# Eight-core hybrid decoder: list-scheduled engines, tiled input and output, block-Toeplitz convolution, folded pooling maps, sums of squares on GpSimd

## The chip, the cores and the metric

The kernel runs on the 8 cores of one Trainium2 chip. Each core handles one sequence of the batch (2048 tokens of 1024 channels), with no exchange between cores. The metric is the device time of the slowest core, in microseconds (us). Each core has TensorE (PE, with the weight loads as PEld), VectorE (DVE), ScalarE (ACT), GpSimd (POOL) and SyncE (SP). They run their own instruction streams and meet through semaphores.

The programs of this case have a second, slower state: in some executions some cores show a lower granted TensorE clock and take longer. In one execution of the kernel before, for instance, cores 4 to 7 had a clock of 0.80 and took 4486 to 4497 us; the other four had 0.966 to 0.971 and took 3822 to 3835.

## The reference, cut to what matters

```python
def reference(x, ...):                         # x (8, 2048, 1024) float32, one sequence per core
    for i in range(4):                         # mixers in order A, B, C, A
        h = rmsnorm(x, norm_mix[i])            # x / sqrt(mean(x*x) + eps) * g
        x = x + mixer[i % 3](h)
        x = x + channel_mlp(rmsnorm(x, norm_mlp[i]), m_w1[i], m_w2[i])   # relu(h@w1)^2 @ w2, 1024->4096->1024
    return rmsnorm(x, norm_final)
# A: z = gelu(h @ w_in + b_in), u and v of 3072 each; v = layernorm(v);
#    gate = causal 128x128 map in chunks of 128 tokens, 8 groups; (u * gate) @ w_out
# B: p = h @ w_in; trailing means over 2, 4, 8, 16 tokens minus p; a 256x256 map per group; @ w_out
# C: a, g = h @ w_in; y = a * sigmoid(g); causal depthwise convolution, 31 taps; layernorm; silu; @ w_out
```

Nine norms of the whole sequence are needed, each in four tiles of 512 tokens. Each of these 36 tile norms stands before some matmuls.

## The kernel before

x stays in SBUF for the whole program, transposed (channels on partitions), as 8 blocks `kc` times 4 tiles `tt` of 128x512 float32. PE transposes x at the beginning and the result at the end. The order of the work is the order of the program text, with look-ahead placed by hand. A tile norm sums its squares on PE: ACT squares a block into bf16, and a matmul with a matrix of 1/1024 adds it up in PSUM (the accumulation memory that matmuls write) and spreads it over all partitions.

```python
def rms_rstd(rb, tt, dst=None, dst_res=None):
    # ... (cut)
    for kc in range(KC):                                      # 8 blocks
        sq, sqr = next_sq()
        sc.op("act", I("activation", out=sq[:], in_=xT[:, kc, t0:t0 + 512], func=AF.Square), ...)
        sc.op("pe", I("matmul", bk[:], lhsT=onesm[:], rhs=sq[:], start=(kc == 0), stop=(kc == KC - 1)), ...)
    sc.op("act", I("activation", out=sd, in_=bk[:], func=AF.Sqrt, bias=epst[:, 0:1], scale=1.0), ...)
    sc.op("dve", I("reciprocal", out=sd, in_=sd), rd=[], wr=[sdr])

def rmsnorm(rb, tt, gcol, out_fn, out_res_fn):
    sd, sdr = rms_rstd(rb, tt)
    for kc in range(KC):                                      # both inputs, x and sd, lie in SBUF
        sc.op("dve", I("scalar_tensor_tensor", out=o, in0=xT[:, kc, t0:t0 + 512],
            scalar=pv[:, gcol + kc:gcol + kc + 1], in1=sd, op0=ALU.mult, op1=ALU.mult), ...)

# mixer A, V: 8 matmuls and a ninth for the bias, then gelu on ACT
fns.append(I("matmul", bk[:], lhsT=sel1[:], rhs=brow[:, vp * 512:(vp + 1) * 512], start=False, stop=True))

# mixer C, convolution: 31 matmuls with diagonal matrices per 128 channels and 512 tokens
fns = [I("matmul", bk[:], lhsT=dg[di][:, k, :], rhs=yext[:, dc, 2 + k:2 + k + 512], start=(k == 0), stop=(k == CK - 1))
       for k in range(CK)]
# ... (input transposes, mixer B, MLP, layer norm of C cut)
```

## Time and profile before

Five runs had a median of 3835.2 us; four lie between 3832.8 and 3838.1, and one took 4102.9. The page of the profile (busy time of each engine, share of the span, instructions) and its chain of work that ended last begin so:

```profile
PE 3595.2 (94%) x16792; PEld 1640.7 (43%) x16792; DVE 2160.1 (56%) x2926; ACT 1069.8 (28%) x1627; POOL 242.6 (6%) x293
...
PE 84%; DVE 7%; ACT 3%; issue 3%; DMA 3%; DVEq 0%; ACTq 0%; SPq 0%; POOLq 0%
```

PE is the bound: 94% busy and 84% of the chain. GpSimd is nearly idle. The next lines are the windows of the slowest core: from:to and length in us, then busy time and instructions of each engine, the granted TensorE clock, the DMA share and the GB/s. They show the start, the first mixer A, the first MLP, mixer B and mixer C.

```profile
0.00:83.00 83.00, 38.44 (x197) 30.80 (x197) 35.03 (x39) 19.27 (x32) 7.34 (x30) 0.76 0.83 174
83.00:652.00 569.00, 553.86 (x2807) 259.49 (x2807) 257.19 (x395) 206.12 (x269) 72.34 (x78) 0.98 0.94 127
652.00:1128.00 476.00, 463.67 (x2101) 206.51 (x2100) 306.14 (x438) 109.56 (x177) 14.29 (x17) 0.99 0.26 42
1128.00:1306.00 178.00, 145.17 (x599) 60.42 (x597) 107.30 (x98) 56.81 (x90) 18.12 (x21) 0.89 0.72 105
...
1776.00:2247.00 471.00, 427.28 (x1830) 180.14 (x1829) 264.92 (x206) 137.96 (x214) 19.88 (x23) 0.95 0.34 52
```

"Busy" is not the same as "at the peak". In back-to-back stretches a bf16 matmul of 512 columns starts every 215.8 ns and one of 128 columns every 55.8 ns. Counting every matmul at these durations (and the float32 ones at theirs) gives 3462 us of PE work that cannot shrink while the instructions stay. The other 375 us of the span are waits and slow restarts after waits. (A restart in this trace: after a wait of 2.75 us, 32 matmuls took 8.75 us instead of 7.07. The granted clock was 0.54 in their first 3.4 us and 1.00 again 5 us after they began.) I call the two parts work and waiting.

Groups, by line, engine, operation, tile and shape (busy us, mean ns of one, then idle time before them and its releaser):

```profile
L79 PE MATMUL bank<-c_yext,c_dg_67 128*128 128x512 bf16 x496 | 117.6, 397 | 12.4 <-DVE c_dg_67 L79 12.4
L79 DVE TENSOR_SCALAR m_hT<-xT,pv 128x512 bf16<-128x512 f32 x128 | 53.2, 488 | 0.6 <-ACT rsq_16 L79 0.2 <-ACT rsq_14 L79 0.2
L79 DVE SCALAR_TENSOR_TENSOR hTp_22<-xT,pv,rsd_20 128x512 bf16<-128x512 f32 x64 | 43.1, 746 | 1.1 <-DVE rsd_20 L79 0.3 <-PE bank L79 0.2
```

The first is half of the 992 diagonal matmuls of the convolution. The other two are the scalings of a norm on DVE: 488 ns with one SBUF tile as input, 746 ns with two (x and the reciprocal root).

### The profile page before, as it was taken

What the parts mean: (1) busy time and instruction counts of PE and PEld (TensorE: products, weight loads), DVE (VectorE), ACT (ScalarE), POOL (GpSimd) and SP (SyncE); (2) the same over time, 40 slices, a digit from 0 to 9 for tenths busy, and PEclk for the clock granted to TensorE, in tenths of its full rate; (3) what the DMA queues carried; (4) which work ended last, traced back from release to release, by engine and by line L of the source; (5) the groups of instructions that cost most, each with busy time, mean ns of one, the idle gap of its engine ahead of it and who ended that gap; (6) DMA issues with size and microseconds to landing.
All of it is one profiled execution on the core that took longest, in us unless ns stands there. A gap on an engine that the chain in (4) does not pass through costs nothing.

```text
span 3837.2 us, 48293 instructions; the slowest of 8 cores (3820.4 to 3837.2 us)
## 1 busy us (share of the span) xinstructions
PE 3595.2 (94%) x16792; PEld 1640.7 (43%) x16792; DVE 2160.1 (56%) x2926; ACT 1069.8 (28%) x1627; POOL 242.6 (6%) x293
## 2 busy tenths in 40 slices
PE   5999998999998799999998989999799999899997
PEld 3444444444443244444333434444344444344444
DVE  4446434655567565666455566566544543465656
ACT  2433332211133221112223241112253423221113
POOL 0111111000001000000000000000001111100000
PEclk7999999999999899999999999999899999999999
DMA  7889999121237422224222422222289999912212
GB/s 151 122 117 136 147 133 135 24 45 34 35 58 108 75 34 34 45 39 72 44 34 35 64 44 45 34 34 44 39 121 123 128 154 129 133 23 45 38 19 88
DMA packets 302325, 283.88 MB, mean 74 GB/s; under 512 B 4870, under 2 KB 281478, under 8 KB 302088
## 3 DMA queue, kind: packets, MB, share of 16 engines
q0 software_dynamic: 295104, 262.16, 47.7%
q1 hardware_dynamic: 6988, 18.64, 1.5%
q8 instruction: 143, 2.34, 0.3%
q14 instruction: 90, 0.74, 0.1%
HBM read 534.54 MB, written 8.39 MB: 141 GB/s over the span
## 4 chain that ended last, share of the span: by engine, by line
PE 84%; DVE 7%; ACT 3%; issue 3%; DMA 3%; DVEq 0%; ACTq 0%; SPq 0%; POOLq 0%
PE bank L79 84%; DVE m_hT L79 1%; DMA ring_9<-a_w_out 1%; DVE hTp_22 L79 1%; DVE xT L79 1%; ACT b_pooled L79 0%; DVE c_dg_66 L79 0%; DVE c_rstd L79 0%; DMA xin_31<-x 0%; DVE b_tA L79 0%; DVE rsd_20 L79 0%; ACT rsq_16 L79 0%; DVE c_dg_67 L79 0%; ACT L79 0%; ACT rsq_14 L79 0%
## 5 line engine op out<-in xcount | busy, mean ns | idle before, releaser
L79 DVE TENSOR_TENSOR xT<-bank,xT 128x512 f32<-128x512 f32 x1152 | 787.0, 690 | 434.4 <-PE bank L79 429.8
L79 DVE BATCH_NORM_STATS2 a_stats<-a_v 128x6 f32<-128x512 bf16 x192 | 129.5, 690 | 184.1 <-ACT a_v L79 183.8
L79 PE MATMUL bank<-m_hT,ring_10 128*128 128x512 bf16 x896 | 207.2, 391 | 14.9 <-DVE m_hT L79 13.7
L79 PE MATMUL bank<-m_hT,ring_9 128*128 128x512 bf16 x896 | 204.1, 387 | 6.7 <-DVE m_hT L79 6.7
L79 ACT ACTIVATE a_uT<-bank,pv 128x512 bf16<-128x512 f32 x192 | 129.5, 689 | 203.1 <-PE bank L79 203.0
L79 ACT ACTIVATE a_v<-bank 128x512 bf16<-128x512 f32 x192 | 114.6, 597 | 244.4 <-PE bank L79 244.2
L79 PE MATMUL bank<-m_hT,ring_11 128*128 128x512 bf16 x768 | 174.3, 386 | 7.0 <-DVE m_hT L79 7.0
L79 PE MATMUL bank<-m_hT,ring_12 128*128 128x512 bf16 x768 | 169.7, 379 | 0.0
L79 PE MATMUL bank<-m_hT,ring_13 128*128 128x512 bf16 x768 | 169.7, 379 | 0.0
L79 PEld LDWEIGHTS bank<-m_hT,ring_10 128*128 128x128 bf16 x896 | 89.3, 100 | 127.8 <-issue 29.5
L79 PEld LDWEIGHTS bank<-m_hT,ring_9 128*128 128x128 bf16 x896 | 89.1, 100 | 116.6 <-issue 16.0
L79 PE MATMUL bank<-c_yext,c_dg_67 128*128 128x512 bf16 x496 | 117.6, 397 | 12.4 <-DVE c_dg_67 L79 12.4
L79 ACT ACT_TABLE_LOAD x43 | 55.2, 1283 | 263.7 <-PE bank L79 228.0
L79 PEld LDWEIGHTS bank<-m_hT,ring_11 128*128 128x128 bf16 x768 | 76.1, 99 | 101.2 <-issue 14.0
L79 PE MATMUL bank<-c_yext,c_dg_66 128*128 128x512 bf16 x496 | 112.7, 385 | 5.0 <-DVE c_dg_66 L79 5.0
L79 PEld LDWEIGHTS bank<-m_hT,ring_12 128*128 128x128 bf16 x768 | 75.2, 98 | 90.6
L79 PEld LDWEIGHTS bank<-m_hT,ring_13 128*128 128x128 bf16 x768 | 75.1, 98 | 90.3
L79 ACT ACTIVATE a_v<-a_v,a_nmr,a_sdv 128x3072 bf16<-128x3072 bf16 x32 | 94.3, 2947 | 22.1 <-DVE a_nmr L79 22.1
L79 PE MATMUL bank<-hTp_22,ring_12 128*128 128x512 bf16 x352 | 83.9, 386 | 6.8 <-ACT a_uT L79 6.8
L79 PEld LDWEIGHTS bank<-c_yext,c_dg_67 128*128 128x128 bf16 x496 | 49.7, 101 | 78.2 <-issue 24.3
L79 PE MATMUL bank<-a_uT,ring_9 128*128 128x512 bf16 x360 | 82.6, 379 | 0.0
L79 PE MATMUL bank<-hTp_22,ring_13 128*128 128x512 bf16 x320 | 75.4, 384 | 7.3 <-ACT hTp_22 L79 7.3
(352 smaller groups left out, 5826.1 us busy)
## 6 DMA issues: line engine op xcount, KB each, us to landing
ring_10<-a_w_in POOLq DMA_DIRECT2D x20, 1024.0 KB, 15.2
ring_11<-a_w_in POOLq DMA_DIRECT2D x20, 1024.0 KB, 12.3
ring_12<-a_w_in POOLq DMA_DIRECT2D x20, 1024.0 KB, 16.1
ring_13<-a_w_in POOLq DMA_DIRECT2D x19, 1024.0 KB, 12.8
ring_9<-a_w_in POOLq DMA_DIRECT2D x17, 1024.0 KB, 18.0
ring_10<-m_w POOLq DMA_DIRECT2D x14, 1024.0 KB, 8.7
ring_9<-m_w POOLq DMA_DIRECT2D x13, 1024.0 KB, 8.3
ring_11<-m_w POOLq DMA_DIRECT2D x13, 1024.0 KB, 8.4
```

Source lines behind the costliest of these rows:

```text
L79: return lambda e: getattr(e, _method)(*args, **kwargs)
```

## The change: intent and core of the diff

The kernel was rewritten. The intent: take off PE what another engine can do, shorten what has to stay, and let a scheduler on the host fix the order of each engine's instructions from modelled durations, so that PE rarely waits.

- x and the output come in tiles that are already transposed, so there are no float32 transposes on the chip.
- Sums of squares: ACT squares in float32, GpSimd adds the 8 blocks (7 adds of 128x512), and PE does one float32 matmul.
- The bias of V is a DVE add in PSUM instead of a ninth matmul.
- Convolution as block-Toeplitz matrices: 384 matmuls of 128 columns and 256 bf16 transposes instead of 992 full matmuls. Mixer C's scalings write straight into the order that this needs.
- Mixer B's group map is multiplied into its output map once.
- The normalisation of v goes from ACT to DVE.

```diff
-        for kc in range(KC):                                     # in rms_rstd
-            sc.op("act", I("activation", out=sq[:], in_=xT[:, kc, t0:t0 + 512], func=AF.Square), ...)
-            sc.op("pe", I("matmul", bk[:], lhsT=onesm[:], rhs=sq[:], start=(kc == 0), stop=(kc == KC - 1)), ...)
+        for kc in range(KC):                                     # in sum_squares
+            sc.op("act", I("activation", out=sq[:], in_=xs(kc, tt), func=AF.Square), ...)
+            if kc:
+                last = kc == KC - 1
+                sc.op("pool", I("tensor_tensor", out=acc if last else sacc[:], in0=sacc[:], in1=sq[:], op=ALU.add), ...)
+    sc.op("pe", MM(bk.v(), onesr[:], acc1[:], True, True), ..., cost=c_pe(1), tag="rms")     # in rms
...
-                        fns.append(I("matmul", bk[:], lhsT=sel1[:], rhs=brow[...], start=False, stop=True))
+                        sc.op("dve", I("tensor_tensor", out=bk.v(), in0=bk.v(), in1=bvb[:, vp * 512:(vp + 1) * 512], op=ALU.add), ...)
...
-            for k in range(CK): ... lhsT=dg[di][:, k, :], rhs=yext[:, dc, 2 + k:2 + k + 512]
+            # in words: c_T (128x1536, built from the taps and a mask, half on DVE, half on GpSimd) times transposed y, 128 columns each
...
+    def schedule(self):                                          # in Sched, on the host
+        while done < n:
+            for e in self.ENGS:                                  # of the ops that are ready on each engine
+                ... cand.append((max(rt, t0), i))                # take the one that can start first
+        o.end = s + cost + (0.12 if e == "pe" else 0.06)         # modelled end
```

## The prediction

> **What bounds it now.** The page (part 1) has PE busy for 3595 of 3837 us (94%), and the chain of waits is 84% PE; DVE is at 56%, ACT 28%, POOL 6%. In an MLP stretch (stage windows) 1730 matmuls of 128x512 take 375 us at granted clock 1.00: 216 ns each. Mixer A's 128-column matmuls in a row come at 56 ns. With the program's counts: 15650 full matmuls (3377 us), 768 short ones (43), float32 input/output transposes (64), mixer A's set-up (28): 3512 us of PE work. The other 325 us is waiting or half-clock restarts: V begins only at 82.9 us (timeline), each mixer-to-MLP change loses about 20 us, mixer B about 50 of 181, the second A set-up 25, the tail 30.
>
> **PE work removed** (estimates from those durations)
> - Convolution: 992 full matmuls become 384 of 128 columns plus 256 bf16 transposes: -178 us.
> - Norm sums, 8 matmuls per tile to 1: -51. Mixer C's LN sums: -14.
> - V's 192 bias matmuls go to DVE: -41.
> - float32 transposes go to the host: -64. A set-up: -24. B's group map: -3.
>
> Sum -375: about 3138 us of PE work remain. Nearly all of it was on the critical path.
>
> **Added elsewhere.** DVE gets 192 bias adds (0.69 us) and v's normalisation (ACT took 2.95 us each), and loses memsets and the 4.3 us diagonal builds. GpSimd gets about 250 adds of 128x512. [...] GpSimd also issues the weight loads (0.88 us each) in order.
>
> **Waits that stay or come**
> - Start: x tile 0 (2 MB) lands near 14 us, then squares, adds, 3.35 us reciprocal, 8 scalings of 0.75: V at about 29 us.
> - Tail: the same chain and the store, about 22 us after the last matmul.
> - Mixer C starts only when all tiles are ready; its end (statistics, transposes, re-read of spilled x, an MLP that needs all of x) leaves PE waiting about 25 us.
> - Mixer B about 15, stage changes 3 to 8 each. A tile of mixer A loads 18.9 MB; the backlogged queue moved 157 GB/s (120 us) and PE will need 135, so DMA nearly binds: some us per layer.
>
> A gap of 3 us also costs 1.8 us of half-clock matmuls (32 took 8.75 instead of 7.07 us). Gaps in all about 75.
>
> **Time.** 3138 + 29 + 22 + 75 = 3264: **3265 us, 8 in 10 between 3205 and 3360**. Faster by over 2%: 0.98; within 2%: 0.015; slower: 0.005.
>
> **What would show it.** PE instructions about 15600; PE busy about 3190 us, 97%; matmuls still 216 ns, clock about 0.98; MLP layers about 445 us each; V's first matmul near 29 us; POOL busy from 243 to 600 us or more; mixer C about 235 us (505 before); mixer B under 140 us; DVE busy not above 2300 us.
>
> **What would make it wrong.** [...] in-order GpSimd holding back weight loads; mixer A bound by DMA; mixer C's end serialised on DVE; a static schedule whose modelled order blocks an engine[...].

The sum came to 3138 + 29 + 22 + 75 = 3264. Of the 29, x at 14, the reciprocal of 3.35 and 8 scalings of 0.75 make 23.4; the other 5.6 (squares, adds, the sum on PE) were the author's estimate.

## The result, and the profile after

The kernel after took 3418.9 us (median of five; four runs between 3416.0 and 3419.0) against 3835.2 us. The ratio is 0.891 (95% interval 0.890 to 0.893). A ratio here is the mean time of one kernel's runs over that of the other's runs of the same rounds, so it is not quite the ratio of the medians. Executions over 1.5% slower than the fastest of the same kernel are left out of the means. The direction was right. The time lies 154 us above the predicted 3265 and outside the range (3205 to 3360).

The fifth run, the one that was profiled, took 8749.9 us, with granted clocks of 0.41 to 0.57 on four cores (the other four had 1.00 and took 7591 to 8211 us). The first experiment ran the same kernel again, and the lines below are from that execution (3412.0 us, all cores at clock 0.975 to 0.977).

> The changed kernel once more, unedited, because its only profile fell in an execution of 8750 us with granted clocks down to 0.41. If that execution is a disturbance of the chip, this one takes about 3419 us with a clock of 0.97 on all cores, and its trace shows where the 154 us over the predicted 3265 us lie. If the kernel itself provokes it, it appears here again.

It was fast and correct, so the long execution was a disturbance and not a property of the kernel. The page after (engines, chain):

```profile
PE 3185.4 (93%) x15640; PEld 1480.1 (43%) x15640; DVE 2228.1 (65%) x3222; ACT 913.8 (27%) x1460; POOL 664.8 (19%) x572
...
PE 85%; DVE 6%; issue 4%; POOL 1%; DMA 1%; SPq 1%; ACT 1%; DVEq 0%; POOLq 0%; ACTq 0%
```

PE's busy time fell by 410 us, as predicted, but its share is 93% and not 97%: the span fell by 428 us, and the waits were not nearly gone. The windows of the same stages:

```profile
0.00:84.00 84.00, 22.00 (x77) 9.16 (x78) 22.57 (x26) 24.98 (x39) 37.51 (x50) 0.88 0.98 191
84.00:600.00 516.00, 507.85 (x2629) 241.24 (x2628) 338.58 (x533) 162.05 (x249) 102.23 (x99) 1.00 1.07 142
600.00:1055.00 455.00, 443.56 (x2048) 200.35 (x2046) 296.87 (x408) 109.48 (x181) 59.81 (x56) 1.00 0.27 42
1055.00:1206.00 151.00, 118.44 (x565) 52.15 (x564) 133.09 (x121) 42.53 (x73) 97.91 (x67) 0.88 0.50 77
...
1652.00:1933.00 281.00, 229.07 (x1478) 125.61 (x1479) 184.08 (x369) 92.36 (x153) 89.64 (x53) 0.91 0.35 70
```

Mixer A and the MLP are within reach of their work. The start (84 us), B (151) and C (281) are not; there the granted clock averages 0.88 to 0.91. The clock record of this trace drops to 0.5 around gaps: from 60.8 to 81.3 us, for instance, where PE stood from 56 to 76.5 us. The waits of PE, by what ended them (us in total, times, longest):

```profile
PE bank L159 <- POOL acc L159: 44.7, 9, 24.7
PE bank L159 <- DVE xT L159: 25.6, 8, 6.8
PE bank L159 <- DVE hT L159: 23.2, 2, 15.3
PE bank L159 <- ACT a_v L159: 20.4, 1, 20.4
PE bank L159 <- DVE c_h L159: 20.3, 1, 20.3
PE bank L159 <- DVE b_pl L159: 19.6, 3, 13.2
PE bank L159 <- DVE c_z L159: 16.7, 2, 15.0
```

The names: `acc` is the GpSimd sum of a norm, `hT` its scaled result, `c_h` the scaled input of mixer C, `a_v` the gelu of V, `b_pl` the pooled tile of B and `c_z` the normalised tile of C. Work and waiting of this trace, counted as before, against the terms of the prediction:

| term | predicted, us | measured, us |
|---|---|---|
| PE work | 3138 | 3135 |
| waiting at the start (predicted: V's first matmul) | 29 | 67 |
| after the last MLP matmul | 22 | 28 |
| waiting in between, restarts included | 75 | 179 |
| sum | 3264 | 3409 |

The 179 us are: mixer A 10 and 23, the MLPs 14, 5, 8 and 12, mixer B 41, mixer C 67. Each figure is the length of a stage less its work. The span of this execution is 3409 us; the median of the five runs is 9 us longer.

Now the groups that answer to those of before (columns as there):

```profile
L159 DVE TENSOR_TENSOR xT<-bank,xT 128x512 f32<-128x512 f32 x1120 | 764.2, 690 | 409.6 <-PE bank L159 397.8
L159 POOL TENSOR_TENSOR sacc<-sacc,sq 128x512 f32<-128x512 f32 x216 | 290.3, 1344 | 262.2 <-ACT sq L159 203.5 <-ACT sacc L159 29.7 <-POOL sacc L159 24.4
L159 DVE SCALAR_TENSOR_TENSOR hT<-xT,pv,rs 128x512 bf16<-128x512 f32 x96 | 98.0, 1086 | 0.3 <-DVE rs L159 0.2
L159 DVE TENSOR_SCALAR mh<-xT,pv 128x512 bf16<-128x512 f32 x128 | 79.8, 652 | 2.7 <-DVE xT L159 0.5
L159 PE MATMUL bank<-c_T,c_yT 128*128 128x128 bf16 x384 | 26.2, 231 | 5.4 <-POOL c_T L159 5.4
```

The new convolution is as short as predicted. But the scalings of the same shape went from 746 to 1086 ns (`hT`) and from 488 to 652 (`mh`, before `m_hT`). These are means of two kinds. Counted one by one in this trace, the 54 `hT` scalings with no GpSimd instruction beside them took 742 ns, and the 42 with one took 1529 ns. For `mh` it is 478 ns (79) and 933 ns (49). The residual adds `xT<-bank,xT`, which read one operand from PSUM and one from SBUF, kept their 690 ns, beside GpSimd (688, 225 of them) as alone (692). DVE itself is not slower; in these groups it depends on what the instruction reads and on what runs beside it. A stretch of the start shows how (start us, us, engine, operation, tiles; the first line merges the 8 scalings of a tile):

```profile
29.84 10.61 DVE L159 SCALAR_TENSOR_TENSOR hT<-xT,pv,rs 128x512 bf16<-128x512 f32 x8 [0.17 <-DVE rs L159]
...
34.44 1.47 POOL L159 TENSOR_TENSOR sacc<-sacc,sq 128x512 f32<-128x512 f32 x1 [0.20 <-POOL sacc L159]
```

Of these 8 scalings, five took 1.74 or 1.75 us. Each of the five ended 0.54 or 0.55 us after the GpSimd add beside it ended (the add above ended at 35.91 us, its scaling at 36.46). A stretch of mixer B's timeline shows the same on a very small instruction:

```profile
1079.85 2.26 DVE L159 TENSOR_TENSOR b_t<-b_t,invc 128x2 f32<-128x2 f32 x1
1080.12 1.96 POOL L159 TENSOR_TENSOR b_t<-b_px 128x1054 f32<-128x1054 f32 x1
...
1090.84 0.15 DVE L159 TENSOR_TENSOR b_t<-b_t,invc 128x6 f32<-128x6 f32 x1
```

A DVE instruction on two columns lasted 2.26 us and ended as the GpSimd instruction beside it ended. A like one on six columns, later, took 0.15 us. The profile counts the stretched time as busy time of DVE. I call this stretching *the port*, as the edits below do; the word is only a name, and no run shows what in the chip causes it. The trace shows which instructions it meets: of those with two SBUF inputs, `hT` (742 ns alone, 1529 beside GpSimd) and the two-column one (2.26 us); of those with one, `mh` (478 and 933). It shows one group that it spares: the residual adds, with one operand in PSUM (692 and 688 ns). The GpSimd adds are longer too: 1.46 or 1.47 us for most of those beside the 8 scalings above, 1.27 us for one alone. (By the profile's starts the two-column instruction came 0.27 us before the GpSimd one with which it ended. Spans on GpSimd are rough in a profile, so this line alone does not show which of the two held up the other.) Why `mh`, with one SBUF input, is stretched, no run shows.

### The profile page after: what moved, and what is told of

Its sections match the earlier page's. It is cut to its first block, busy times and chain, and to the rows that moved or that the text cites. A ratio compares the mean times of both kernels' runs of the same rounds, so it can differ in the third digit from the quotient of the medians.

```text
span 8748.3 us, 45371 instructions; the slowest of 8 cores (6789.2 to 8748.3 us)
## 1 busy us (share of the span) xinstructions
PE 8645.4 (99%) x15640; PEld 2691.2 (31%) x15640; DVE 2240.3 (26%) x3222; ACT 925.1 (11%) x1460; POOL 645.6 (7%) x572
## 4 chain that ended last, share of the span: by engine, by line
PE 99%; DVE 1%; issue 0%; POOL 0%; DMA 0%; ACT 0%; DVEq 0%; SPq 0%; POOLq 0%; ACTq 0%
PE bank L159 99%; DVE xT_43 L159 0%; DVE hT_19_61 L159 0%; DVE c_h_125 L159 0%; POOL sacc_56 L159 0%; DVE rs_16_58 L159 0%; POOL c_T_97_140 L159 0%; DMA xT_43<-x 0%; DVE c_z_104_147 L159 0%; DVE rs_17_59 L159 0%; DVE c_st_128 L159 0%; POOL acc_57 L159 0%; DVE mh_110_153 L159 0%; DVE c_mv_129 L159 0%; ACT rs_16_58 L159 0%
## 5 line engine op out<-in xcount | busy, mean ns | idle before, releaser
L159 DVE TENSOR_TENSOR xT_43<-bank,xT_43 128x512 f32<-128x512 f32 x1120 | 772.8, 691 | 2547.3 <-PE bank L159 2547.3
L159 DVE SCALAR_TENSOR_TENSOR bank<-bank,pv_49,a_S_66 128x512 f32<-128x512 f32 x96 | 72.2, 758 | 459.7 <-PE bank L159 459.3
L159 DVE TENSOR_TENSOR bank<-bank,a_bvb_63 128x512 f32<-128x512 f32 x96 | 67.2, 700 | 472.7 <-PE bank L159 463.2
L159 PE MATMUL bank<-a_uT_70,ring_6_48 128*128 128x512 bf16 x192 | 149.1, 1038 | 0.0
L159 PE MATMUL bank<-a_uT_70,ring_4_46 128*128 128x512 bf16 x192 | 148.9, 1038 | 0.0
L159 PE MATMUL bank<-a_uT_70,ring_5_47 128*128 128x512 bf16 x192 | 148.8, 1036 | 0.0
L159 DVE SCALAR_TENSOR_TENSOR bank<-bank,pv_49,a_S_149 128x512 f32<-128x512 f32 x96 | 71.8, 757 | 259.6 <-PE bank L159 259.6
L159 DVE TENSOR_TENSOR bank<-bank,a_bvb_169 128x512 f32<-128x512 f32 x96 | 67.2, 700 | 248.2 <-PE bank L159 248.2
L159 ACT ACTIVATE a_v_62<-bank 128x512 bf16<-128x512 f32 x96 | 56.8, 599 | 659.8 <-DVE bank L159 659.8
L159 ACT ACTIVATE a_uT_70<-bank,pv_49 128x512 bf16<-128x512 f32 x96 | 66.2, 689 | 539.8 <-PE bank L159 539.8
L159 POOL TENSOR_TENSOR sacc_56<-sacc_56,sq_13_55 128x512 f32<-128x512 f32 x72 | 93.3, 1296 | 285.1 <-ACT sq_13_55 L159 267.6
L159 ACT ACTIVATE a_v_168<-bank 128x512 bf16<-128x512 f32 x96 | 57.4, 598 | 479.9 <-DVE bank L159 479.9
L159 POOL TENSOR_TENSOR sacc_56<-sacc_56,sq_11_53 128x512 f32<-128x512 f32 x72 | 93.1, 1292 | 157.4 <-ACT sq_11_53 L159 137.6
L159 ACT ACTIVATE a_uT_172<-bank,pv_49 128x512 bf16<-128x512 f32 x96 | 66.2, 690 | 345.8 <-PE bank L159 345.7
L159 POOL TENSOR_TENSOR sacc_56<-sacc_56,sq_12_54 128x512 f32<-128x512 f32 x72 | 92.5, 1285 | 131.9 <-ACT sq_12_54 L159 96.0
L159 PEld LDWEIGHTS bank<-a_wmb_67,a_v_62 128*128 128x128 bf16 x384 | 71.8, 207 | 92.8 <-issue 88.7
L159 PE MATMUL bank<-a_uT_172,ring_3_45 128*128 128x512 bf16 x192 | 97.5, 720 | 0.0
L159 PE MATMUL bank<-a_uT_172,ring_2_44 128*128 128x512 bf16 x192 | 97.5, 722 | 0.0
L159 PE MATMUL bank<-a_uT_172,ring_6_48 128*128 128x512 bf16 x192 | 97.5, 720 | 0.0
L159 PE MATMUL bank<-a_wmb_67,a_v_62 128*128 128x128 bf16 x384 | 95.0, 461 | 0.0
L159 PE MATMUL bank<-ring_6_48,c_h_125 128*128 128x512 bf16 x128 | 76.4, 833 | 12.2 <-DVE c_h_125 L159 12.2
```

The lines of the kernel that those rows point to most:

```text
L159: return lambda e: getattr(e, _method)(*[_r(a) for a in args], **{k: _r(v) for k, v in kwargs.items()})
```

## The experiments

Theory P, in short: the PE work is as predicted, and the missing time is waits of PE. The largest part of them comes from GpSimd's adds, in two ways: the chain square, add, matmul is long (7 adds of 1.27 us and more), and DVE's scalings take longer beside the adds (1529 ns against 742). Smaller parts come from places where the fixed order makes PE wait for work that it doesn't need yet. The rivals, named in the expectations, say that these waits are harmless, or that the added DVE work or the scheduler's order as a whole sets the time. Times are against 3419 us of the kernel after, unless I say otherwise.

### 1. The adds made thin

Each add of a norm, except mixer C's, touches 16 columns instead of 512. The result is wrong; the instructions and their order stay nearly the same.

```diff
-    sum_squares(tt, acc1[:], acc1_r)
+    sum_squares(tt, acc1[:], acc1_r, cut=16)     # adds: sacc[:, 0:16] += sq[:, 0:16]
```

> Theory P (the port): the extra waiting comes from GpSimd's 512-column adds, through their serial chain and because they stretch DVE instructions with two SBUF inputs (hT 1.09 us on average against 0.75 before, c_h 1.26 against 0.65 when GpSimd is idle). Here the adds of all norms but mixer C's touch 16 columns, same order, same count (the result is wrong on purpose). P expects hT back at 0.75 us, mh back at 0.49 us, first V matmul before 31 us, and a gain of 60 to 100 us. Theory S (the static order and the serial stages, whatever GpSimd does) expects under 30 us.

Measured: 3359.0 us (four runs within 2.1 us), ratio 0.876 against 0.891. The adds, with all that follows from their length, cost about 60 us. That is at the low end of what P expected. The groups of this run, and two lines of its timeline (PE at the start, as in experiment 3):

```profile
L159 DVE SCALAR_TENSOR_TENSOR hT<-xT,pv,rs 128x512 bf16<-128x512 f32 x96 | 69.1, 788 | 0.3 <-DVE rs L159 0.2
L159 POOL TENSOR_TENSOR sacc<-sacc,sq 128x16 f32<-128x16 f32 x192 | 49.3, 257 | 329.4 <-ACT sq L159 277.5 <-ACT sacc L159 44.4 <-POOL sacc L159 4.5
...
28.75 10.01 PE L159 MATMUL bank<-ring,hT 128*128 128x512 bf16 x32 [10.05 <-DVE hT L159]
...
76.51 3.75 PE L159 MATMUL bank<-a_ws,onesf 128*128 128x512 f32 x4 [23.87 <-ACT a_v L159]
```

With thin adds the same scaling took 788 ns instead of 1086, and V's first matmul came at 28.75 us instead of 40.70: within 0.3 us of the predicted 29. `mh` fell to 552 ns, not to the 490 that P expected.

The earlier first matmul gained little where it happened. PE then waited 23.9 us for the gate's weights (experiment 3) and went on at 76.51 us, where the kernel after goes on at 76.52. To see where a gain lies, I cut the traces into stages, each MLP from its first matmul on `mh` to its last on `aT`. On the eight cores of the kernel after, each stage but the first has the same length to 1 us. The start with the first mixer A got 3 us shorter here; the other 51 us of this pair of traces lie later (12 in mixer B, 13 in the second mixer A, 18 in the MLPs).

### 2. The sums back on PE

The opposite trade: 8 bf16 matmuls per tile norm again, no GpSimd adds (C's stay).

```diff
-        sum_squares(tt, acc1[:], acc1_r)
-        sc.op("pe", MM(bk.v(), onesr[:], acc1[:], True, True), ...)
+        for kc in range(KC):
+            sc.op("act", I("activation", out=sq, in_=xs(kc, tt), func=AF.Square), ...)        # sq in bf16
+            sc.op("pe", MM(bk.v(), onesb[:], sq, kc == 0, kc == KC - 1), ...)                 # onesb = 1/1024
```

> The squares of all norms but mixer C's are bf16 again and summed by 8 matmuls instead of GpSimd adds and 1 matmul: 32 norms x 7 x 0.216 = 48 us more PE work. If P holds, waiting falls by about as much as in the thin run and the time is within 30 us of the changed kernel (3385 to 3440); if S holds, it is 35 to 50 us longer.

Measured: 3421.2 us (three runs within 0.8 us; the fourth was slow), ratio 0.892. PE's line of the page:

```profile
PE 3235.5 (95%) x15864; PEld 1499.4 (44%) x15864; DVE 2166.6 (63%) x3223; ACT 918.3 (27%) x1468; POOL 367.9 (11%) x348
```

PE got 48 us more work (3183 against 3135 by the count) and the time rose by about 2 us. So in this kernel moving the sums to GpSimd was, in sum, worth almost nothing: it took 48 us of work off PE and gave nearly all of it back as waits.

The stages show that this small sum has two large parts. The four MLP stages took 36 us longer, for 34 us more PE work: there the move had been worth its full size. All other stages together (start, mixers, tail) took 27 us less, although their PE work rose by 14 us; 17 of the 27 lie in the second mixer A. (The two profiled executions, on two chips, differ by these 9 us; the median of the kernel after lies 7 us above its profiled execution. On every core the MLPs took 33 to 36 us longer and the rest 19 to 37 us less.)

### 3. The gate's weights loaded first

At the start the SP queue loads x, and after it the small gate weights `a_ws`. ACT's fixed order has the copy of these weights before the first gelu. When the eight banks of PSUM were full, after 64 matmuls, PE waited for that gelu (20.4 us). The kernel after's timeline (`a_ws` was issued after the x loads; PE stood from 56 to 76.5 us):

```profile
40.19 10.27 SPq L159 DMA_DIRECT2D a_ws<-a_w_sT  x1
40.70 15.45 PE L159 MATMUL bank<-ring,hT 128*128 128x512 bf16 x64 [15.27 <-DVE hT L159]
76.52 3.75 PE L159 MATMUL bank<-a_ws,onesf 128*128 128x512 f32 x4 [20.36 <-ACT a_v L159]
```

```diff
-                        self.setup(uoff, after=first_x[-1:])
+                        self.setup(uoff)
```

> The load of the gate matrix (a_ws, 0.5 MB) is issued before x tiles 1 to 3 instead of after them. If the 20.4 us wait at 56 us comes from ACT's fixed order (the copy of a_ws stands before the first gelu and its data landed at 72 us), that wait goes and the time falls by 15 to 21 us. If weights or the bias row bound the start anyway, it falls by less than 5 us.

Three of five runs were slow and the other two differ by 17 us (3404.0 and 3421.2), so I compare cores whose clock was not lowered: 3392 to 3398 us, where the kernel after had 3402 to 3410 (on another chip). That is about 10 us, between the two expectations of 15 to 21 and under 5. The 20.4 us wait became one of 7.1 us, but V's first matmul still waited for `hT`, until 41.62 us. The stages settle where the gain lies: on an undisturbed core (core 2) the start with the first mixer A took 585 us, against 591 to 598 on the cores of the kernel after, and every later stage kept its length to within about 1 us. So the gain is real and is between 6 and 14 us.

### 4. The scheduler told about the port

In the scheduler's model, listed kinds of DVE and GpSimd instructions now exclude each other, and the hand-over times are those read from traces (in the lines above: 0.17 us from `rs` to `hT` on DVE, 0.20 us from one GpSimd add to the next). A stricter rule for spare banks had to come with it, or the scheduler found no order at all, so this is not a pure test.

```diff
+                    if o.tag in (PORT_DVE if e == "dve" else PORT_POOL if e == "pool" else ()):
+                        rt = max(rt, port[e])
...
-                o.end = s + cost + (0.12 if e == "pe" else 0.06)
+                o.end = s + cost + LATENCY.get(e, 0.06)          # pe 0.33, act 0.17, dve 0.17, pool 0.2
```

> Same work; only the list scheduler's model changes: [...] the time from an engine's end to the next engine's start is set as measured (0.33 us after PE, 0.17 to 0.2 after the others, instead of 0.12 and 0.06). If the order[...] is what loses, 30 to 60 us are gained; if the port itself is, under 15 us, or a loss.

Two runs (3441.1, 3442.3) had one pair of cores at clock 0.958 that set the time; two more were slow. The cores at 0.974 or above took 3376 to 3395 us, which is some 10 to 25 us less than in the kernel after. The result lies between the expectations of P (30 to 60) and of the rival (below 15), and I count it as inconclusive: a better-informed order helps somewhat, but it can't remove the adds.

### 5. The scalings read the reciprocal from PSUM

The square root and its reciprocal stay in the PSUM bank in which the sum was made. `hT` and the final scalings then have one SBUF input and one PSUM input instead of two SBUF inputs, as the residual adds have, which kept their 690 ns beside GpSimd. The adds stay. The bank is now held until the eight scalings are done, so the schedule shifts somewhat too.

```diff
-        if dst is None:
-            t, (r,) = rsb[rbn[0] % 2]
-            dst = (t[:], r)
+        if dst is None:
+            dst = (bk.v(), bk)
```

> Only the place of the reciprocal changes: for the mixers' norms and the final norm it stays in its PSUM bank, so the eight scalings that follow read one SBUF and one PSUM operand instead of two SBUF operands. The GpSimd adds stay as they are. If DVE instructions with two SBUF inputs wait for GpSimd (theory P), the hT group falls from 1.09 to about 0.75 us, the adds beside it from about 1.45 to 1.27, and 15 to 35 us of the 60 that the thin adds gained come back. If the length of the GpSimd chain alone cost those 60 us, hT may shorten but the time falls by less than 8 us.

Measured: 3383.7 and 3384.8 us in the two fast runs (the two others were slow), on the chip on which the kernel after took 3412.0: 28 us less there, 35 less than the median of 3419. P is supported. The groups:

```profile
L159 DVE SCALAR_TENSOR_TENSOR hT<-xT,pv,bank 128x512 bf16<-128x512 f32 x96 | 64.3, 739 | 0.2 <-DVE bank L159 0.2
L159 POOL TENSOR_TENSOR sacc<-sacc,sq 128x512 f32<-128x512 f32 x216 | 285.6, 1322 | 256.8 <-ACT sq L159 193.7 <-ACT sacc L159 29.0 <-POOL sacc L159 23.7
```

The scaling is back from 1086 to 739 ns with all adds in place: 67 of the 96 had a GpSimd instruction beside them and took 739 ns, the same as the others (738). The adds beside them fell from 1427 to 1272 ns, as expected; the group's mean fell only from 1344 to 1322, because most adds run beside something else. `mh` and `c_h` were not changed and kept 658 and 1262 ns. By stages, 15 of the 27 us between the two profiled executions lie in the second mixer A and 7 in mixer B. So about half of the 60 us of experiment 1 comes from the stretching of these scalings, up to what the shifted schedule adds or takes, and a few lines avoid it. (The expectation lay between 15 and 35.)

### 6. Program order instead of list order

The same kernel, but each engine takes its instructions in the order in which the program text makes them.

```diff
                 for i in avail[e]:
+                    if i != rest[e][-1]:
+                        continue
```

> The same program, but every engine issues in the order in which the program was written; the list scheduler only assigns PSUM banks. The chip's waits tell what the list order is worth: if it hides the norms, the V bias and the gate chain behind PE, the time rises by 150 us or more, with PE waiting for DVE hT, ACT and GpSimd at each stage; if PE's work alone made the gain, it rises by less than 50 us.

Measured: 3970.9 us (3969.1 to 4007.6), ratio 1.035 (1.027 to 1.043). The list order is worth about 550 us against this text order. In its own text order the new code, with all its removed PE work, is slower than the kernel before. Page and the first of PE's waits, from the profiled execution of 4007.6 us:

```profile
PE 3315.1 (83%) x15640; PEld 1516.6 (38%) x15640; DVE 2235.8 (56%) x3222; ACT 895.6 (22%) x1440; POOL 652.8 (16%) x572
...
PE bank L159 <- POOL acc L159: 347.3, 29, 29.5
```

PE waited 347 us for the GpSimd sums alone, in 29 waits. The sums' chain is long. The list order leaves 44.7 us of these waits. The kernel before also runs in text order, but with look-ahead placed by hand and with its sums on PE; no run separates these two, so the 550 us are not the worth of a scheduler over a hand-made order.

### 7. The bias of V back on PE

```diff
-    [MM(bk.v(), hT[...], wv[:, kc, :], kc == 0, kc == KC - 1) for kc in range(KC)]
-    sc.op("dve", I("tensor_tensor", out=bk.v(), in0=bk.v(), in1=bvb[...], op=ALU.add), ...)
+    [MM(bk.v(), hT[...], wv[:, kc, :], kc == 0, False) for kc in range(KC)] + [MM(bk.v(), onesb[:], bvb[...], False, True)]
```

> The kernel after, with one removed piece of TensorE work put back: the bias of V is again a ninth matmul of each of the 192 accumulations (an all-1/128 matrix times the bias row that lies in all 128 partitions), and the DVE bias add between the matmuls and the gelu is gone. The added TensorE work is 192 x 216 ns = 41.5 us. Theory P (the time of the kernel after is the TensorE work plus waits that others cause, so work taken off TensorE was worth its full size in mixer A): 3448 to 3465 us, that is +32 to +48 us, with the waits of PE on DVE in mixer A a few us smaller at most. Rival R1 (DVE and not PE sets the pace of mixer A's V stretch since it got the bias add, so the removal was worth little): less than +15 us. The matmuls of V go from 1536 to 1728 in the groups.

Measured: 3458.1 us (three runs between 3456.2 and 3458.5; one with a pair of cores at 0.964 took 3483.9), ratio 0.903. The group of the added matmuls:

```profile
L159 PE MATMUL bank<-a_bvb,onesb 128*128 128x512 bf16 x192 | 73.0, 380 | 0.0
```

192 matmuls of 216 ns are 41.5 us, and the time rose by 39. By stages, the second mixer A got 18.5 us longer for 20.7 us more work, and the start with the first mixer A 25.8 us for 20.7; nothing else changed by more than about 1 us. (At the start V's first matmuls now come only at 78.4 us, since each accumulation needs the bias row, whose load is issued after x.) Here removed PE work was worth its full size. The contrast with experiment 2: the bias add replaced a matmul by a DVE instruction that reads one PSUM operand, and with the matmul put back PE's waits changed by only about 5 us in all. The sums replaced matmuls by a chain of GpSimd adds of 1.27 us and more that, outside the MLPs, PE then waits for (44.7 us on `acc`) and beside which DVE's scalings are stretched (1529 ns against 742).

### 8. Mixer C's entry

Half of the `c_h` scalings go to ACT, and the last Toeplitz builds go from GpSimd to DVE (the modelled cost of DVE's builds is raised with it).

```diff
             for kc in range(KC):
+                if kc % 2:
+                    sc.op("act", I("activation", out=h[...], in_=xs(kc, tt)..., func=AF.Copy, scale=pv[...]), ...)
+                    continue
...
-                        eng = "pool" if k % 2 else "dve"
+                        eng = "pool" if k % 2 and Q < 3 else "dve"
```

> The kernel after, changed in mixer C alone: half of the scalings that rearrange x for C (c_h) go to ACT instead of DVE, and the last quarter's Toeplitz builds (c_T) are all on DVE, none on GpSimd. Theory P (the entry of C waits 20.3 us on the serial DVE scalings c_h of the last token tile[...]): the wait on c_h falls from 20.3 to 8 to 13 us, C as a whole gets 8 to 15 us shorter, total 3399 to 3411 us. The 15.0 us wait on c_z at C's end stays, because bn_aggr, square root and the first c_z remain one serial chain. Rival: the entry wait is set by the last residual adds and not by c_h; then the wait stays above 16 us and the total within 4 us of the kernel after.

Only one run of four was undisturbed: 3399.4 us. A second one took 3423.0 us, with one pair of cores at 0.968 or 0.969 (3420 us) and the others at 3386 to 3395; two were slow. The cores of the undisturbed run took 3390 to 3397, where those of the kernel after took 3402 to 3410: about 13 us. In the kernel after the wait was 20.3 us on `c_h`. Here:

```profile
PE bank L159 <- DVE c_z L159: 16.6, 2, 14.7
...
PE bank L159 <- ACT c_h L159: 6.7, 1, 6.7
```

The wait fell by the size of the gain, and `c_z` at the other end of C stayed, as expected. The mean `c_h` on DVE fell from 1264 to 740 ns: one of 16 took about 1.66 us, where 17 of 32 had taken 1.65 us or more. No run separates the two edits.

### 9. The parts together

The edits of 3, 5 and 8 at once, and with them: the first and the last tile norm sum on PE, half of the MLP scalings run on ACT, the load of V's bias row is issued earlier, and x tiles load one tile ahead.

> The repairs together, same schedule rules: gate matrix first, x tiles 1 to 3 loaded one tile ahead instead of at once, scalings from PSUM, half of the mh and c_h scalings on ACT, the first and last norm summed by PE (idle there), mixer C's last diagonal builds on DVE. If the causes named (port, start, tail, mixer C's start) are right they add: 12 us from the gate load as measured, 15 to 35 from the port, about 10 each from start, tail and mixer C: 3330 to 3370 us. If they hide one another, it stays above 3380.

Measured: 3330.4 us in the undisturbed fast run, with all cores between 3325 and 3329; another at 3337.6 had one pair of cores slightly lower; two were slow. Inside the expected 3330 to 3370. With the port model of experiment 4 added to the scheduler:

> The combined version, its schedule made with the port and the measured hand-over times as in the port run, which gained about 19 us on cores whose clock was not disturbed. [...] within 15 us of the combined version; if the order is still a cause of its own, 15 to 30 us faster.

Measured: 3322.7, 3326.6 and 3328.7 us in three fast runs of four, ratio 0.865 (0.856 to 0.874), 2 to 8 us below the undisturbed run without the port model on the same chip. (The port should matter less here; the `hT` scalings took 737 ns.) The gain is inside the expected 15 us, and too little to call the order a cause of its own. Its chain:

```profile
PE 90%; DVE 3%; issue 3%; DMA 2%; POOL 1%; ACT 1%; SPq 0%; DVEq 0%; POOLq 0%; ACTq 0%
```

The chain is 90% PE, after 85% in the kernel after. The same kernel once more, on another chip, with five rounds:

> The same kernel as s6l_combined_port, run again with five rounds, because the first time (3322.7 and 3327.7 us in two fast runs of three) gave a wide interval. Expected: fast runs between 3318 and 3332 us, ratio to before 0.864 to 0.869, and at most half of the runs disturbed.

(The expectation quotes the earlier times inexactly; they are the three given above.) It failed: the five fast runs took 3345.4 to 3378.7 us, ratio 0.874 (0.871 to 0.878). In each of them at least one pair of neighbouring cores had a clock of 0.964 to 0.974, and that pair set the time. The cores at 0.979 or above took 3313 to 3325 us, as on the first chip. So the version is faster than both kernels on either chip, by about 13% of the time before and 2 to 3% of that after. How much of the last few microseconds is left depends on the granted clock, which differed between executions of this one kernel (the lowest core had 0.964 to 0.973 in these five, 0.979 to 0.981 in the three on the first chip). What lowers it is not shown: the thin-adds kernel, nearly as dense by PE's share (95% against 96%), had 0.977 to 0.980 in all four runs on the same chip.

## Why the prediction was right or wrong

**Right: the bound and the PE work.** Predicted 3138 us of work, measured 3135. Instructions 15640 (about 15600 predicted), PE busy 3185 (3190), matmuls still at 216 ns, clock 0.976 (0.98), MLP layers 445 to 455 us (about 445), POOL busy 665 (600 or more), DVE busy 2228 (not above 2300). (The GpSimd add alone took 1.27 us; the estimate of it is cut.)

**Right: mixer A was not bound by DMA.** No DMA is among the ten largest waits of PE (the tenth is 9.5 us).

**Wrong: the step "Gaps in all about 75", with the start at 29.** Waiting in between was 179 us, the start 67, the tail 28 instead of 22. That is 148 of the 154 us. The prediction had put its estimate of the add chain under the 13.8 us of an MLP tile step (64 matmuls of 216 ns) and taken the sums as free everywhere. What the runs showed in its place:

- *Norm sums, -51.* This term of the removed work was counted at full value. In the MLP stages, where the comparison with the tile step applies, it was right: experiment 2 took 36 us longer there for 34 us of work. It failed for the sums at the start, in the mixers and at the tail: there the work came off PE and came back as waits, and with the sums back on PE these stages took 27 us less. In the second mixer A, where 17 of these 27 lie, experiment 5 alone wins back 15, with the adds in place and the scalings freed: there it was mainly the port. In the other stages the causes are not separated. In all, experiment 2 puts the sums back for 2 us, and experiment 1 puts the price of the adds at 60 us.
- *The port.* The prediction expected such a stretching in mixer B alone, from no run. It showed wherever a norm's scalings run beside another tile's adds, which in the list order happened to 42 of the 96 `hT` scalings: 1086 ns instead of 746 on average. Experiment 5 puts 28 to 35 us on it. It had been allowed for in one stage only.
- *Start.* V at 40.7 us instead of 29. The first sum reached PE at 24.66 us (17.93 with thin adds), and then the first tile's 8 scalings ran beside the second tile's adds and took 10.61 us, against 8 x 0.746 = 6.0. Experiment 1, free of both, gives 28.75 us. Then came 20.4 us behind the gate's weights, which the prediction did not see; experiment 3 wins back about 10 us. The two waits hide each other: with thin adds alone PE went on at the same 76.5 us, and with the gate's weights first V still waited for `hT` until 41.62 us. With both removed (experiment 9, with its other edits) the start with the first mixer A is 32 to 37 us shorter.
- *Mixer C, "about 25" of waiting, 235 us in all.* 67 and 281. At the entry 20.3 us on `c_h`, of which experiment 8 takes 13 away. The 15.0 us on `c_z` at its end and the 13.2 us on B's first pooled tile were expected in kind; no run changed them alone.

These parts overlap (the port also stretches `c_h`, 1.26 us on average against 0.65 alone), so they must not be added up. Together, experiment 9 takes away about 93 us of the 154. The other 60 or so are not traced one by one; the 14.7 us on `c_z` and, without the port model, the 13.2 us on B's first pooled tile are still there in experiment 9.

**Named as a risk, and it happened:** "a static schedule whose modelled order blocks an engine" (experiments 3 and 4) and "mixer C's end serialised on DVE"; and GpSimd making DVE and the norms late (`hT` 1086 ns instead of 746). Naming them without putting a number on them left the range too narrow. The granted clock in the fast runs of the kernel after (0.972 to 0.977) was not below that of the kernel before (0.966 to 0.969 in its profiled execution).

**Wrong in the same way:** mixer B took 151 us (under 140 predicted), and PE's share was 93% instead of 97%.

## What to carry to other kernels

Work that leaves the bound engine is worth its full size only if nobody waits longer for its new place: put one such move back alone, as experiments 2 and 7 do, and the two kinds come apart at once (2 us against 39). Then compare stage by stage: a small difference in all can be two large ones, here 36 us more in the MLPs and 27 us less elsewhere. Before GpSimd gets elementwise work, list the DVE instructions that will run beside it and read SBUF alone: here the scalings among them took about twice as long beside it (`hT` 742 and 1529 ns, `mh` 478 and 933). Reading one operand from PSUM took `hT` off that list (739 ns beside it, 738 alone). And when a static order is computed on the host, look at the few longest waits of the bound engine in the trace: here each was an instruction queued ahead of one it had nothing to do with, or a serial chain at a stage's edge.
